# Splitting the first up- and down-weights of the ConvFFN two segments early, and moving the mixer's weight stores to GpSimd's queue

## The chip, the cores and the metric

The kernel runs on one core of one Trainium2 chip. The metric is the device time of one execution in microseconds (us). Three executions of the kernel before took 2495.51, 2503.52 and 2504.46 us; the median is 2503.52 us.

## The reference

One layer of a hybrid decoder over 2048 prompt columns and 8 sample columns, D_MODEL = 1024, D_FF = 2816, all in float32. Cut to what matters:

```python
h  = rms_norm(x, norm1) * (1 + sc1) + sh1
proj = h @ w_in                      # q, k, v | z | beta, alpha | u, v of the gating MLP
q, k, v = silu(causal_dwconv(proj_qkv, width 4))
o_a, S = gated_delta_rule(q, k, v, g, beta, s0)      # chunks, triangular solve, scan over the state S
o_a = rms_norm(o_a) * silu(z)
o_b = gelu(u) * (W_s @ rms_norm(gelu(vb)) + b)       # 128x128 mixing inside chunks
x  = x + g1 * (concat(o_a, o_b) @ w_out)
h2 = rms_norm(x, norm2) * (1 + sc2) + sh2
up = causal_dwconv(h2 @ w_up, width 3) + b
x  = x + g2 * ((silu(up[:, :D_FF]) * up[:, D_FF:]) @ w_down)
y  = rms_norm(x, final_norm)
```

## The kernel before

**Products.** A float32 product is made of three float32r products: each operand is split into a high part (a copy that rounds to float32r) and a low part (the rest). `split` does that with one ScalarE copy (L100) and one VectorE subtraction (L97). `gemm_steps` issues the three matmuls of a 128-row step on lines L119, L120 and L121. A split weight block is a tile of 128 x 2 x 512, 512 KB, high and low side by side.

**Kept weights.** A weight block is split once. `wblock(key, w, src)` splits it into the tile `w` and stores the tile to DRAM (L166, on SyncE's queue, called SP in the profile); whenever the same key comes again it loads the kept block instead (L162, on GpSimd's queue, called POOL). Segment 0 of the mixer splits all of `w_in` (48 blocks) and `w_out` (16 blocks); block 0 of the ConvFFN splits all of `w_up` and `w_down`.

**Mixer.** Four segments of 512 columns, counted 0 to 3 (segment 0 has the 8 sample columns beside them). Each one runs, in the order in which the program is written: the 12 q, k, v tiles of the input projection (`qkv_tile`) with convolution and the triangular solve (`solve_steps`, `solve_merge`); the sgu stage, four heads with one u tile and one v tile each (`sgu`, `sgu_norm`, `sgu_post`); the weave, in which the four z tiles of the projection are laid between the four steps of the state scan (`weave`, `scan`, with L575, L582, L588 and L597 to L598 as the products of a step and L579, L585 and L592 as the work between them); `gdn_post`; the load of the next segment's x (L327, SP's queue), its squares and their sum (L345, L347), a reduction over the 128 partitions by eight small products with a vector of ones (L188), the reciprocal root (`rstd_of`, L182) and its broadcast (L199); and the output projection `out_proj` with the residual stored for later (L683, L692).

**ConvFFN.** Three column blocks of 688, 688 and 680 columns. In each, 22 up-projection pairs (a gate tile and a value tile) are computed with seven half-width products of 12 matmuls a piece, on the weight blocks B11, B21, T1, T2, B22, T3, T4 of a pair. `up_weights` takes them from DRAM if they are kept; otherwise it loads 2 x 512 KB raw (L153), makes four sums and differences (L974 and the lines behind it) and splits seven blocks. After every second or third pair a down round (`down`, two blocks per down tile) adds to the output. Before the first pair, `load_h2` makes the moving operands of the first column block from the stored h2: 16 additions and subtractions of 128 x 344 (L944, L945, L951, L952) on GpSimd where `early` is set, on VectorE otherwise, and 14 splits.

**Order.** The program is built under a tile context with a scheduler that simulates a timeline and orders the instructions of every engine by it, so what is written at one place can be issued at another. Each engine then works in that order, and so does each DMA queue's issuing engine: an issue that waits for a semaphore holds up what stands behind it on that engine. GpSimd's transfers use eight semaphore lanes, so that one issue also waits until the one eight places earlier has landed. Tiles come from pools with a fixed number of buffers; an instruction that writes a tile waits until the last reader of the buffer is done. The `w` blocks have 6 buffers, the `wb` blocks of the up-projection 6, `sv` 3 and `cv` 4.

Of the kernel before, what the change touches and what calls it, by code (L numbers as in the profile page):

```python
# [9 lines left out]
F32 = mybir.dt.float32  # L10
F32R = mybir.dt.float32r
BF16 = mybir.dt.bfloat16
AF = mybir.ActivationFunctionType
ALU = mybir.AluOpType
# [11 lines left out]
FT = 22  # L26
# [19 lines left out]
def trunk(ctx, tc, A, O):  # L46
# [108 lines left out]


    kept = {}

    def wblock(key, w, src=None):

        if key in kept:
            G.dma_start(out=w, in_=kept[key])  # L162
        else:
            split(w[:, 0], w[:, 1], src)
            kept[key] = dr.tile([128, 2, 512], F32, name="kept_" + "_".join(map(str, key)))
            nc.sync.dma_start(out=kept[key], in_=w.bitcast(F32))  # L166
        return [(w[:, 0, k * 128:(k + 1) * 128], w[:, 1, k * 128:(k + 1) * 128]) for k in range(4)]

    def wpt():
# [45 lines left out]
    def nm():  # L215

        return po.tile([128, 520], F32, tag="nm", name="nm", bufs=3)
# [89 lines left out]
    def cv_slabs():  # L307
        while True:
            yield cv()[:, 0:512]
# [615 lines left out]
    def load_h2(c0, W, early=False):  # L925

        n = W // 2
        X, rest = {}, []
        eng = G if early else V
        for k in range(4):  # L930
            if k < 3 or not early:
                p, q = acct(), rawt()
# [196 lines left out]
                out=O["yT"][k * 128:(k + 1) * 128, c0 + b0:c0 + b0 + n], in_=x)  # L1129


    c = nm()[:, 0:72].rearrange("p (k c) -> p k c", k=8)
    nc.scalar.dma_start(out=c, in_=A["cT"])
    V.memset(cact, 0.0)
# [62 lines left out]
    for s in range(NSEG):  # L1197
# [36 lines left out]
        mix = mix[4:] + mix[:4]  # L1234
        pend = None
        extra = mod_half(4, cv_slabs()) if s == 0 else iter(())
        for hd in range(4):
            uv = uvt()
            sgu(0, hd, uv, h, W, extra)
            with behind():  # L1240
                if hd:
                    sgu_norm(pend)
                else:
                    v_head(3, vf[3], Z)
            sgu(1, hd, uv, h, W, extra)
            with behind():
                if hd:
                    sgu_post(hd - 1, pend, W, mix)
                else:
                    solve_merge(Z)  # L1250
            pend = uv
            if s == 0 and hd == 2:
                sk = smp_conv()
                vn, o_s, eg_s = smp_delta(sk, Z["beta"], Z["g"], states)
# [9 lines left out]
        state = Z["S"]  # L1264
        if s == 0:
            smp_mix(mix, 0, smp_gate(o_s))
        gdn_post(Z, z, W, mix)
        if s == 0:
            scale_of(s2, 32, "norm2")
# [27 lines left out]
            h2, rest = load_h2(*CB[0], early=True)  # L1297
        sq = out_proj(range(5, KT), *last, x1, acc)
        if s + 1 == NSEG:
            w0 = up_weights(0)  # L1300
        norm_h2(x1, *last[:2], (acc, sq))
    sto.close()
# [140 lines left out]
```

## Time and profile before

| | |
|---|---|
| median of three executions | 2503.52 us |
| the profiled execution's own time | 2499.25 us |
| its span, first to last instruction | 2496.5 us |
| ConvFFN block 0 (first product to the first product of block 1) | 1048.4 to 1532.8 us of the span |
| ConvFFN block 1 | 1532.8 to 1995 us |
| weave of segments 1 and 2 | some 465 to 513 and 705 to 752 us |

Times inside the profile are microseconds from the span's start. PE is TensorE's matmul stream, DVE VectorE, ACT ScalarE, POOL GpSimd, SP SyncE; a name with a q behind it (SPq) is that engine's issuing of DMAs. "Waits" are idle time of an engine just before an instruction, put down to the instruction or transfer that released it last. The granted clock (PEclk) is a share of 2.4 GHz; its low level is 1.2 GHz. GB/s is what the core's 16 DMA engines moved.

### The profile page before, as it was taken

What the parts mean: (1) busy time and instruction counts of PE and PEld (TensorE: products, weight loads), DVE (VectorE), ACT (ScalarE), POOL (GpSimd) and SP (SyncE); (2) the same over time, 40 slices, a digit from 0 to 9 for tenths busy, and PEclk for the clock granted to TensorE, in tenths of its full rate; (3) what the DMA queues carried; (4) which work ended last, traced back from release to release, by engine and by line L of the source; (5) the groups of instructions that cost most, each with busy time, mean ns of one, the idle gap of its engine ahead of it and who ended that gap; (6) DMA issues with size and microseconds to landing.
All of it is one profiled execution on the core that took longest, in us unless ns stands there. A gap on an engine that the chain in (4) does not pass through costs nothing.

```text
span 2496.5 us, 41843 instructions
## 1 busy us (share of the span) xinstructions
PE 2414.7 (97%) x15770; PEld 2240.9 (90%) x15770; DVE 1713.3 (69%) x3731; ACT 1045.9 (42%) x2128; POOL 501.3 (20%) x769
## 2 busy tenths in 40 slices
PE   7899999999999999999999999999999999999997
PEld 4798978888887878889999998999999999999997
DVE  4675668455745664799899998766655685666655
ACT  5766655456445645454444444412222242222223
POOL 0000001111201211311111112333333223333333
PEclk9999999999999999999999999999999999999998
DMA  9785787566737754888787778977777778767773
GB/s 377 243 282 170 255 306 212 153 194 202 209 113 223 222 163 143 305 327 307 280 298 295 284 287 302 319 225 237 240 228 223 223 233 296 225 212 231 227 238 116
DMA packets 224057, 600.84 MB, mean 241 GB/s; under 512 B 39345, under 2 KB 67697, under 8 KB 223345
## 3 DMA queue, kind: packets, MB, share of 16 engines
q0 software_dynamic: 84672, 308.32, 39.8%
q1 hardware_dynamic: 128672, 278.83, 31.6%
q10 hardware_dynamic: 10512, 11.04, 1.3%
q8 instruction: 124, 2.03, 0.3%
q14 instruction: 77, 0.62, 0.1%
HBM read 430.39 MB, written 167.70 MB: 240 GB/s over the span
## 4 chain that ended last, share of the span: by engine, by line
PE 75%; DVE 12%; DMA 7%; issue 3%; ACT 2%; SPq 0%; POOL 0%; ACTq 0%; DVEq 0%; POOLq 0%
PE u L119 9%; PE u L120 9%; PE u L121 9%; PE g L119 7%; PE g L120 7%; PE g L121 7%; PE d L119 6%; PE d L120 6%; PE d L121 6%; DVE acc L1021 1%; DVE cv L376 1%; DVE wb L97 1%; DVE sv L508 1%; DMA S<-in_w_down 1%; DVE TP L506 1%
## 5 line engine op out<-in xcount | busy, mean ns | idle before, releaser
L119 PE MATMUL g<-hh,w 128*128 128x512 f32 (+1 forms) x960 | 346.4, 361 | 7.7 <-ACT w L100 7.7
L1021 DVE SCALAR_TENSOR_TENSOR acc<-raw,vec,acc 128x680 f32<-128x680 f32 (+1 forms) x264 | 303.5, 1152 | 70.0 <-ACT acc L1014 67.6
L119 PE MATMUL d<-midh,w 128*128 128x344 f32 (+1 forms) x1008 | 322.2, 325 | 22.1 <-DVE xa L1087 11.9
L119 PE MATMUL u<-T,wb 128*128 128x344 f32 (+1 forms) x1056 | 338.1, 321 | 4.9 <-DMA wb<-kept_w_up_T 2.4
L121 PE MATMUL g<-hh,w 128*128 128x512 f32 (+1 forms) x960 | 341.6, 356 | 0.0
L120 PE MATMUL g<-hl,w 128*128 128x512 f32 (+1 forms) x960 | 340.6, 355 | 0.0
L120 PE MATMUL u<-T,wb 128*128 128x344 f32 (+1 forms) x1056 | 338.4, 321 | 0.3 <-DVE T L97 0.3
L121 PE MATMUL u<-T,wb 128*128 128x344 f32 (+1 forms) x1056 | 337.2, 320 | 0.9 <-DVE wb L97 0.9
L120 PE MATMUL d<-midl,w 128*128 128x344 f32 (+1 forms) x1008 | 323.7, 322 | 0.0
L121 PE MATMUL d<-midh,w 128*128 128x344 f32 (+1 forms) x1008 | 317.4, 322 | 0.4 <-DVE w L97 0.4
L1087 DVE SCALAR_TENSOR_TENSOR xa<-d,mod,xa 128x344 f32<-128x344 f32 (+2 forms) x368 | 206.1, 568 | 153.7 <-PE d L121 144.8
L1014 ACT ACTIVATE acc<-raw,vec 128x680 f32<-128x680 f32 (+1 forms) x132 | 125.9, 956 | 383.7 <-DVE raw L1009 379.1
L119 PE MATMUL u<-B,wb 128*128 128x344 f32 (+1 forms) x792 | 252.6, 320 | 2.7 <-ACT B L100 2.7
L120 PE MATMUL u<-B,wb 128*128 128x344 f32 (+1 forms) x792 | 253.1, 320 | 0.2
L121 PE MATMUL u<-B,wb 128*128 128x344 f32 (+1 forms) x792 | 252.0, 318 | 0.0
L162 POOL DMA_DIRECT2D w<-kept_w_in x144 | 76.2, 529 | 718.0 <-PE g L121 379.4
L119 PEld LDWEIGHTS d<-midh,w 128*128 128x128 f32 x1008 | 191.6, 191 | 26.6 <-issue 11.5
L119 PEld LDWEIGHTS g<-hh,w 128*128 128x128 f32 x960 | 182.9, 191 | 35.1 <-ACT w L100 8.6
L121 PEld LDWEIGHTS g<-hh,w 128*128 128x128 f32 x960 | 182.2, 190 | 28.1 <-issue 2.8
L120 PEld LDWEIGHTS g<-hl,w 128*128 128x128 f32 x960 | 182.9, 191 | 26.7 <-issue 2.0
L119 PEld LDWEIGHTS u<-T,wb 128*128 128x128 f32 x1056 | 199.4, 189 | 6.1 <-DVE sacc L1100 2.1
L121 PEld LDWEIGHTS u<-T,wb 128*128 128x128 f32 x1056 | 199.7, 189 | 1.3 <-DVE wb L97 1.2
(391 smaller groups left out, 5063.4 us busy)
## 6 DMA issues: line engine op xcount, KB each, us to landing
wb<-kept_w_up_T POOLq DMA_DIRECT2D x176, 512.0 KB, 5.0
w<-kept_w_in POOLq DMA_DIRECT2D x144, 512.0 KB, 4.0
wb<-kept_w_up_B POOLq DMA_DIRECT2D x132, 512.0 KB, 4.9
kept_w_up_T<-wb SPq DMA_DIRECT2D x88, 512.0 KB, 4.0
w<-kept_w_down POOLq DMA_DIRECT2D x88, 512.0 KB, 5.0
kept_w_up_B<-wb SPq DMA_DIRECT2D x66, 512.0 KB, 4.1
kept_w_in<-w SPq DMA_DIRECT2D x48, 512.0 KB, 4.2
w<-kept_w_out POOLq DMA_DIRECT2D x48, 512.0 KB, 4.4
```

What stands on the lines that cost most here:

```text
L97: (eng or V).tensor_tensor(out=out, in0=a, in1=hi.bitcast(F32), op=ALU.subtract)
L119: PE.matmul(ps[:, :n], wh, mh[:, c0:c0 + n], start=k == ks[0], stop=False)
L120: PE.matmul(ps[:, :n], wh, ml[:, c0:c0 + n], start=False, stop=False)
L121: pe["last"] = PE.matmul(ps[:, :n], wl, mh[:, c0:c0 + n], start=False, stop=k == ks[-1])
L162: G.dma_start(out=w, in_=kept[key])
L376: V.scalar_tensor_tensor(out=acc, in0=cr[:, j:j + SEG], scalar=vc("cqkv", ft * 4 + j), in1=acc, op0=ALU.mult, op1=ALU.add)
L506: V.tensor_tensor(out=tmp, in0=NB[:, j, j + 1:32].unsqueeze(2).to_broadcast([64, r, w]), in1=TB[:, j:j + 1, 0:w].to_broadcast([64, r, w]), ...
L508: V.tensor_tensor(out=TB[:, j + 1:32, 0:w], in0=TB[:, j + 1:32, 0:w], in1=tmp, op=ALU.subtract)
L1014: S_.activation(out=acc[:, off:W], in_=raw[:, 2:2 + m], func=AF.Identity, scale=vc("cffn", ft * 3 + 2), bias=vc("cffb", ft))
L1021: V.scalar_tensor_tensor(out=acc[:, off:W], in0=raw[:, j:j + m], scalar=vc("cffn", ft * 3 + j), in1=acc[:, off:W], op0=ALU.mult, op1=ALU.add)
L1087: V.scalar_tensor_tensor(out=xa[ft][:, b0 + o:b0 + n], in0=ps[:, o:n], scalar=mod[:, 40 + ft, 0:1], in1=xa[ft][:, b0 + o:b0 + n], op0=ALU. ...
```

## The change

Three edits. First, the stores of kept blocks go to the queue named in `keeper`: GpSimd's from the start, SP's again from just before the first `up_weights` of the ConvFFN; so 48 + 16 stores of segment 0 change their queue. Second, `prepare(s)` in segments 1 and 2 loads, adds, splits and keeps the weights of two up pairs and two down tiles each (pairs and tiles 0 and 1 in segment 1, 2 and 3 in segment 2): per segment 3 MB raw in on SP's queue, into four `cv` tiles a pair; 8 sums and differences; 18 blocks split (18 ScalarE copies and 18 VectorE subtractions) into `sv` tiles of the name `wv`; and 18 stores of 512 KB on GpSimd's queue. Four of its eight steps are written into heads 2 and 3 of the sgu stage, the rest behind the weave. Block 0 of the ConvFFN then finds these 36 blocks kept and loads them on GpSimd's queue, where it had loaded 6 MB raw, split 36 blocks and stored them. Third, the 16 additions of `load_h2` for block 0 are on VectorE (`eng = V`).

```diff
     kept = {}
+    keeper = {"q": G}
...
-            nc.sync.dma_start(out=kept[key], in_=w.bitcast(F32))
+            keeper["q"].dma_start(out=kept[key], in_=w.bitcast(F32))
...
-        eng = G if early else V
+        eng = V
...
+    def prep_block(key, src):
+        wblock(key, pa.tile([128, 2, 512], F32R, tag="sv", name="wv", bufs=3), src)
+
+    def prep_up(i):
+
+        a11, a12, a21, a22 = (cv()[:, 0:512] for _ in range(4))
+        for j, (p, q) in enumerate(((a11, a12), (a21, a22))):
+            for n, a in enumerate((p, q)):
+                nc.sync.dma_start(out=a, in_=A["w_up"][j * FT + i][:, n * 512:n * 512 + 512])
+        key = lambda n: ("w_up", i, n)
+        prep_block(key("B11"), a11)
+        prep_block(key("B21"), a12)
+        prep_block(key("T4"), a22)
+        yield
+        V.tensor_tensor(out=a22, in0=a21, in1=a22, op=ALU.add)
+        prep_block(key("T1"), a22)
+        V.tensor_tensor(out=a21, in0=a11, in1=a21, op=ALU.subtract)
+        prep_block(key("T3"), a21)
+        yield
+        V.tensor_tensor(out=a11, in0=a22, in1=a11, op=ALU.subtract)
+        prep_block(key("T2"), a11)
+        V.tensor_tensor(out=a12, in0=a12, in1=a11, op=ALU.subtract)
+        prep_block(key("B22"), a12)
+        yield
+
+    def prep_down(i):
+        for j in range(2):
+            a = cv()[:, 0:512]
+            nc.sync.dma_start(out=a, in_=A["w_down"][i][:, j * 512:j * 512 + 512])
+            prep_block(("w_down", i, j), a)
+        yield
+
+    def prepare(s):
+
+        if s in (1, 2):
+            for i in (2 * s - 2, 2 * s - 1):
+                yield from prep_up(i)
+                yield from prep_down(i)
...
+        ready = prepare(s)
         for hd in range(4):
+            if hd > 1:
+                next(ready, None)
             uv = uvt()
             sgu(0, hd, uv, h, W, extra)
...
+            if hd > 1:
+                next(ready, None)
             sgu(1, hd, uv, h, W, extra)
...
+        for _ in ready:
+            pass
         gdn_post(Z, z, W, mix)
...
         if s + 1 == NSEG:
+            keeper["q"] = nc.sync
             w0 = up_weights(0)
```

Line numbers behind the first edit are higher by one in the changed kernel (L163 is the kept load, L167 the store), and higher by more behind the new functions. PE has the same products as before.

On POOL, at the end of segment 1's projection, only loads of kept blocks stood (`w_in_14_1` is half 1 of tile 14 of `w_in`; the numbers behind a name count the tiles of the program):

```order
L162 DMA w_5941<-kept_w_in_14_1_3186 128x1024
L162 DMA w_6021<-kept_w_in_15_0_3298 128x1024
L162 DMA w_6023<-kept_w_in_15_1_3303 128x1024
L162 DMA w_6185<-kept_w_out_0_0_3513 128x1024
L162 DMA w_6187<-kept_w_out_0_1_3518 128x1024
L162 DMA w_6218<-kept_w_out_1_0_3583 128x1024
```

Now the stores of split blocks stand between the same loads (here those of pair 1 and down tile 1):

```order
L163 DMA w_6084<-kept_w_in_15_1_3303 128x1024
L167 DMA kept_w_up_1_B11_6124<-wv_6121 128x1024
L167 DMA kept_w_up_1_B21_6129<-wv_6126 128x1024
L167 DMA kept_w_up_1_T4_6134<-wv_6131 128x1024
L163 DMA w_6307<-kept_w_out_0_0_3513 128x1024
L167 DMA kept_w_up_1_T1_6140<-wv_6137 128x1024
L167 DMA kept_w_up_1_T3_6146<-wv_6143 128x1024
L167 DMA kept_w_up_1_T2_6152<-wv_6149 128x1024
L163 DMA w_6309<-kept_w_out_0_1_3518 128x1024
L167 DMA kept_w_up_1_B22_6158<-wv_6155 128x1024
L167 DMA kept_w_down_1_0_6165<-wv_6162 128x1024
L163 DMA w_6340<-kept_w_out_1_0_3583 128x1024
```

A store waits for its split on VectorE and a load for a `w` buffer that PE gives free; each of them now holds up the other kind.

On PE, behind the scan of segment 1, the sums of the next segment's squares (`c<-ones,nm`) were followed by 25 rows of the output projection (`g<-mh,w`) before the broadcast of the root (`c<-ident,rtok`):

```order
L188 MATMUL c_6115<-ones_74,nm_6112 128x1
L119 MATMUL g_6190<-mh_5216,w_6185 128x512
L120 MATMUL g_6190<-ml_5217,w_6185 128x512
L121 MATMUL g_6190<-mh_5216,w_6185 128x512
...
L119 MATMUL g_6190<-mh_5222,w_6185 128x512
L199 MATMUL c_6127<-ident_72,rtok_6124 128x128 x4
L120 MATMUL g_6190<-ml_5223,w_6185 128x512
```

Now eight rows stand between them:

```order
L189 MATMUL c_6237<-ones_74,nm_6234 128x1
L120 MATMUL g_6312<-ml_5219,w_6307 128x512
L121 MATMUL g_6312<-mh_5218,w_6307 128x512
L119 MATMUL g_6312<-mh_5220,w_6307 128x512
L120 MATMUL g_6312<-ml_5221,w_6307 128x512
L121 MATMUL g_6312<-mh_5220,w_6307 128x512
L119 MATMUL g_6312<-mh_5222,w_6307 128x512
L120 MATMUL g_6312<-ml_5223,w_6307 128x512
L121 MATMUL g_6312<-mh_5222,w_6307 128x512
L200 MATMUL c_6249<-ident_72,rtok_6246 128x128 x4
```

The broadcast comes 17 rows sooner behind the sums; the sums themselves stand 61 products behind the scan's last one, where they stood 64 to 66 behind.

On POOL, at the end of the mixer, the loads of the last `w_out` tiles stood between additions of `load_h2`, and nothing of the up-weights:

```order
L162 DMA w_10543<-kept_w_out_3_1_3831 128x1024
L944 TENSOR_TENSOR mc_10623<-acc_10617 128x344
L945 TENSOR_TENSOR mc_10624<-raw_10618,mc_10623 128x344
L951 TENSOR_TENSOR acc_10617<-raw_10618,acc_10617 128x344
L162 DMA w_10576<-kept_w_out_4_0_3938 128x1024
```

Now six blocks of pair 0 come at that place, the first down blocks and the seventh block of pair 0 behind `w_out`, and pair 1 after them:

```order
L163 DMA wb_11077<-kept_w_up_0_B11_5540 128x1024
...
L163 DMA w_11045<-kept_w_out_7_1_4435 128x1024
L163 DMA w_11551<-kept_w_down_0_0_5722 128x1024
...
L163 DMA wb_11089<-kept_w_up_0_T4_5550 128x1024
L163 DMA wb_11306<-kept_w_up_1_B11_6124 128x1024
L163 DMA wb_11308<-kept_w_up_1_B21_6129 128x1024
L163 DMA wb_11310<-kept_w_up_1_T1_6140 128x1024
L163 DMA wb_11312<-kept_w_up_1_T2_6152 128x1024
```

The load of `kept_w_up_1_B11` waits until PE has read the buffer of the first pair's second block, and PE has 24 matmuls and seven small sums between that and its first use.

## Rows read from the trace of the kernel before

**Rows 1.** The page: busy time, its share of the span and the number of instructions of each engine; the granted clock in 40 slices of the span.

```profile
PE 2414.7 (97%) x15770; PEld 2240.9 (90%) x15770; DVE 1713.3 (69%) x3731; ACT 1045.9 (42%) x2128; POOL 501.3 (20%) x769
PEclk9999999999999999999999999999999999999998
```

**Rows 2.** PE's waits from 400 to 1000 us, which hold segments 1, 2 and most of 3: who waited for whom, us in total, times, the longest.

```profile
PE c L531 <- DMA lt<-td: 3.6, 2, 2.2
PE c L473 <- DVE A L476: 2.0, 2, 1.7
```

**Rows 3.** Windows: length, busy us (and instructions) of PE, PEld, DVE, ACT and POOL, the granted clock, the DMA engines' share and GB/s. The first is pairs 0 to 3 of ConvFFN block 0, the second a stretch of block 1 with PE never idle, then the whole of block 0 and of block 1.

```profile
1048.40:1130.50 82.10, 75.36 (x458) 73.59 (x457) 78.89 (x165) 44.37 (x74) 10.07 (x7) 0.96 0.92 344
1700.00:1800.00 100.00, 100.00 (x639) 100.00 (x638) 64.01 (x103) 20.62 (x29) 32.91 (x56) 1.00 0.75 235
1048.40:1532.80 484.40, 461.44 (x2864) 457.45 (x2862) 447.73 (x903) 217.52 (x350) 67.75 (x53) 0.98 0.82 302
1532.80:1995.00 462.20, 458.00 (x2917) 456.16 (x2916) 305.37 (x539) 118.05 (x182) 145.06 (x240) 1.00 0.76 244
```

**Rows 4.** PE's four longest waits from 1048.4 to 1130.5 us (two shorter ones follow them).

```profile
PE d L119 <- ACT w L100: 2.4, 1, 2.4
PE u L119 <- DVE mc L1027: 1.7, 1, 1.7
PE u L121 <- DVE wb L97: 0.9, 1, 0.9
PE c L199 <- DVE rtok L182: 0.9, 1, 0.9
```

**Rows 5.** Groups by line and form from 1042 to 1110 us, ACT and then DVE: busy us, mean ns of one, idle before.

```profile
L100 ACT ACTIVATE wb<-S 128x512 fp32r<-128x512 f32 x12 | 7.5, 629 | 11.1 <-DVE S L981 3.9 <-PE u L121 2.5 <-DVE S L984 1.7
L97 DVE TENSOR_TENSOR wb<-S,wb 128x512 fp32r<-128x512 f32 x12 | 8.4, 703 | 0.0
```

**Rows 6.** The page's groups: the first product of the up-projection in all three blocks, with PE's idle time before it.

```profile
L119 PE MATMUL u<-T,wb 128*128 128x344 f32 (+1 forms) x1056 | 338.1, 321 | 4.9 <-DMA wb<-kept_w_up_T 2.4
```

**Rows 7.** The page's DMA issues: KB each and median us from issue to landing.

```profile
wb<-kept_w_up_T POOLq DMA_DIRECT2D x176, 512.0 KB, 5.0
w<-kept_w_in POOLq DMA_DIRECT2D x144, 512.0 KB, 4.0
kept_w_up_T<-wb SPq DMA_DIRECT2D x88, 512.0 KB, 4.0
```

**Rows 8.** Groups from 1010 to 1046 us, the stretch in which `load_h2` runs: POOL, then DVE beside it, then two DVE groups of the same shapes from 1480 to 1600 us; then the window 1010 to 1046 us.

```profile
L951 POOL TENSOR_TENSOR acc<-raw,acc 128x344 f32<-128x344 f32 x3 | 3.1, 1030 | 0.0
L97 DVE TENSOR_TENSOR B<-raw,B 128x344 fp32r<-128x344 f32 x6 | 6.6, 1120 | 0.0
L97 DVE TENSOR_TENSOR T<-mc,T 128x344 fp32r<-128x344 f32 x8 | 5.6, 696 | 0.0
L97 DVE TENSOR_TENSOR B<-acc,B 128x344 fp32r<-128x344 f32 x3 | 4.4, 1477 | 0.0
...
L97 DVE TENSOR_TENSOR T<-mc,T 128x344 fp32r<-128x344 f32 x16 | 7.8, 506 | 0.0
L97 DVE TENSOR_TENSOR B<-raw,B 128x344 fp32r<-128x344 f32 x8 | 4.6, 581 | 3.6 <-ACT B L100 3.5
...
1010.00:1046.00 36.00, 35.87 (x155) 28.71 (x154) 29.16 (x39) 14.63 (x32) 20.70 (x25) 1.00 0.84 274
```

**Rows 9.** Windows with the columns of rows 3: the weave of segment 1, the stretch behind it, the ten microseconds before the x loads at segment 1's end, and six microseconds at the start of the ConvFFN.

```profile
465.00:513.00 48.00, 48.00 (x339) 42.70 (x340) 18.61 (x43) 22.35 (x61) 4.75 (x9) 1.00 0.42 122
513.00:530.00 17.00, 17.00 (x86) 14.09 (x85) 10.46 (x29) 11.96 (x24) 2.64 (x5) 1.00 0.92 320
500.00:510.00 10.00, 10.00 (x69) 9.09 (x68) 2.19 (x6) 4.51 (x18) 0.53 (x1) 1.00 0.18 54
1050.00:1056.00 6.00, 5.90 (x43) 5.82 (x41) 6.00 (x16) 5.44 (x12) 0.00 (x0) 1.00 1.03 415
```

**Rows 10.** The timeline of POOL before 526 us (start, length, instruction, idle before it and its releaser), of SP's issue of x, of ACT's last square, of DVE's last sum and of PE's sums and broadcast.

```profile
502.93 0.53 POOL L162 DMA_DIRECT2D w<-kept_w_out  x1 [6.72 <-PE g L121]
510.22 0.53 POOL L162 DMA_DIRECT2D w<-kept_w_out  x1 [6.76 <-PE g L121]
511.76 2.25 SPq L327 DMA_DIRECT2D x<-in_xT  x4
526.05 0.62 ACT L345 ACTIVATE nm<-x 128x512 f32<-128x512 f32 x1
530.16 1.06 PE L188 MATMUL c<-ones,nm 128*128 128x1 f32 x9
537.32 1.05 PE L199 MATMUL c<-ident,rtok 128*128 128x128 f32 x8
```

**Rows 11.** The last line of the tile view of x from 500 to 548 us: us from issue to landing.

```profile
DMA to landing us min/median/max: 6.5/8.2/11.4
```

**Rows 12.** A group of DVE from 483 to 513 us, the scan of segment 1.

```profile
L592 DVE SCALAR_TENSOR_TENSOR S<-S,ed,c 128x128 f32<-128x128 f32 x16 | 4.5, 343 | 11.6 <-PE c L588 11.6
```

**Rows 13.** Waits from 0 to 300 us, segment 0: SP's largest, and PE's two largest.

```profile
SPq L166 <- DVE w L97: 94.0, 26, 13.4
PE m L266 <- ACT cact L1135: 13.0, 1, 13.0
PE g L119 <- ACT w L100: 7.7, 1, 7.7
```

## Prediction

> **What bounds the kernel now.** The first view is the page's busy times: PE works 2414.7 us of the 2496.5 us span, 97%, and its granted clock is at the high level in every slice but the last [rows 1]. So a change pays only where PE waits or runs at the low clock, and costs wherever it makes PE wait. PE's waits come next. From 400 to 1000 us, where the new work of segments 1 and 2 is put, two lines wait for 5.6 us in all [rows 2]. There is next to nothing to win there, and whatever the new work disturbs is lost. The windows of the ConvFFN show the place that can win: block 0 has PE idle for 484.40 - 461.44 = 23.0 us, block 1, which runs on kept blocks, for 462.20 - 458.00 = 4.2 us [rows 3]. Segment 0 has two long waits on other things [rows 13].
>
> **Pairs 0 to 3 of block 0.** They take 82.1 us for 458 matmuls. In a stretch of block 1 in which PE is never idle one matmul takes 100 / 639 = 0.1565 us, and 458 of them 71.7 us; 10.4 us are lost. The four longest waits are 2.4 on ScalarE's split, 1.7 and 0.9 behind VectorE, and 0.9 on the reciprocal root, 5.9 us [rows 4]; the granted clock of 0.96 is worth 0.04 x 82.1 = 3.3 us [rows 3]; the rest are small waits. VectorE is busy 78.89 of the 82.1 us, so all those waits stand behind a full queue. The change takes 36 splits of 0.70 us (25 us) and 16 sums of that size (11 us) from VectorE and 36 copies of 0.63 us (23 us) from ScalarE here [rows 5], so VectorE is left near half busy and 5.9 us of waits go. What is late next are the loads. Blocks 1 and 2 take every weight in this way, and the first product of theirs and of block 0 waits for such a load 2.4 us in all [rows 6], a small price; but at the start there is no lead: pair 1's first load waits for the buffer of pair 0's second block, and has 24 matmuls (24 x 0.1565 = 3.8 us) and seven sums before it is needed, against a landing of 5.0 us [rows 7]. I take 1 us. Raw loads and stores of the old way were 1.5 + 4.5 = 6 MB a pair, loads of the new way are 4.5 MB, and the DMA engines, at a share of 0.92 there, get easier. The clock I leave as it is, since new waits may bring it down as the old ones may have. The small waits are the rest, 10.4 - 5.9 - 3.3 = 1.2 us, and go with the others: -5.9 - 1.2 + 1 = -6. The ends are -10.4, when clock and waits both go, and -5.9 + 2 x 5.0 = +4, when pairs 0 and 1 each wait a whole landing.
>
> **The 16 additions.** VectorE takes 16 x 0.51 = 8.1 us more. But beside GpSimd's additions its own subtractions took 1.12, 0.70 and 1.48 us where the same shapes took 0.58, 0.51 (and, for the third, I take 0.58 too) later: 6 x 0.54 + 8 x 0.19 + 3 x 0.90 = 7.5 us come back [rows 8]. VectorE had 29.16 of 36 us busy there and PE 35.87. Zero, from -1 to +2. The Trainium skill ("SBUF — State Buffer", section "Who interferes with whom") says that the two engines share a port pair under an exclusive lock; the 1.12 us beside 0.58 agree with it. Without that rule the move would cost up to the 8 us that it adds to a VectorE with 7 us idle, some 1 us of PE.
>
> **Segments 1 and 2.** Each stores 18 x 0.52 = 9.4 MB and loads 3.1 MB raw. VectorE gets 18 splits and 8 sums at 0.70 us, 18 us, in a weave of 48 us where it is busy 18.6; ScalarE 18 x 0.63 = 11 us beside 22.4. The DMA engines move 122 GB/s there, and 415 GB/s were seen [rows 9], so the bulk fits. Three things may not:
>
> - *The scan.* VectorE waits for PE 11.6 us before its state updates [rows 12]: it is a chain PE, VectorE, PE with z products laid between. Splits stand right before its links, each waiting for a copy by ScalarE, which waits for one of three `sv` buffers, whose store (4.0 us to land [rows 7]) may stand on POOL's queue behind a load that waits for PE: such loads were issued at 502.93 and 510.22 us, after idle times of 6.7 and 6.8 us [rows 10]. Bounds: nothing, and one landing of 4.0 us in each of two steps. I take 1 us, because by POOL's order the stores that a split of pair 1 needs stand behind loads that PE lets go a step earlier.
> - *The x loads.* They are issued from 511.76 us, and took 6.5 to 11.4 us to land [rows 10, 11]. The stretch behind has 0.92 of the DMA engines' time taken at 320 GB/s, while the ten microseconds before had 54 GB/s [rows 9]. The stores of B22 and of the two down blocks, 1.6 MB, go out behind POOL's load at 510.22, so beside x; at 415 GB/s that is 3.8 us. The slack: the last square ended at 526.05 + 0.62 = 526.67, PE's nine sums began at 530.16 [rows 10]; they now come three to five products sooner, some 0.7 us, which leaves 2.8 us. So 1.0 us of wait; the bounds are nothing, and 4.8 us when all six last blocks (3.1 MB, 7.6 us) pass ahead of x.
> - *The root.* From the end of the sums at 531.22 to the broadcast at 537.32 us, 6.1 us, PE had 25 products, 0.24 us each [rows 10]. With eight there are 1.9 us. How long square root and reciprocal take is not to be seen but for its bound, 6.1 us, since PE did not wait: the cost is 0 to 4.2 us; I take 0.5, as the scheduler's rows behind need the result later and x is then on time or late with it.
>
> That is 2.5 us a segment, 5 for both, from 0 to 2 x 17.
>
> **Segment 0.** SP waited 94 us to store split blocks [rows 13], and raw loads stand behind those. They now go ahead. But of PE's long waits the 13.0 us are the start and the 7.7 us wait for a copy by ScalarE, whose order is the same up to there. 48 + 16 stores cost POOL issue slots of 0.53 us [rows 10] where it has little else to do. Zero, between -2 and +2.
>
> **Sum.** -6 + 0 + 5 + 0 = -1 on the profiled 2499.25 us. That execution is 4.3 us under the median of the three, which lie 9 us apart; I carry the difference over to the median, 2503.5 - 1 = 2502.5.
>
> **Rivals.**
>
> 1. *All of the loss at the start of the ConvFFN goes, and the mixer hides everything.* For it: the 14 MB of spare traffic in the weave, 29 us of idle VectorE. Against: the clock, whose dips have no shown cause there. -10.4, and -2 in segment 0: 2503.5 - 12.4 = 2491.
> 2. *Stores in the scan and beside x; slower.* Place: VectorE's splits ahead of the scan's links in segments 1 and 2. Price: two landings of 4.0 us, and 4.8 us for x, 12.8 a segment, 25.6 for both, less 6: 2503.5 + 19.6 = 2523. It decides from the point where a split ahead of a link waits for an `sv` buffer longer than the z products between the links last. For it: VectorE and POOL run in order and both wait for PE; against: the stores have 7 us between two loads of POOL and land in 4. The Trainium skill ("DMA: Bandwidth & Descriptors", section "SWDGE vs HWDGE vs iDMA") speaks for the x part: GpSimd's and SP's transfers go to different queues inside each DMA engine, which takes turns between them, so stores on GpSimd's queue would not wait for x but take a share of it; the landings of 6.5 to 11.4 us of x beside POOL's loads agree.
> 3. *The loads at the start of the ConvFFN come late.* Pairs 0 to 3 keep the time they had or lose 4 us: 2503.5 + 5 + 2 = 2510. For it: 36 loads in 80 us behind one queue whose issue waits for PE's buffers; against: the 2.4 us of rows 6.
> 4. *The splits of pairs 4 and on inherit the waits.* Pair 4 still splits seven blocks; if the pile-up only moves from pairs 0 to 3 to pairs 4 to 7, the gain is nil and the mixer's 5 us stay: 2508. Against: the splitting has 80 us of free VectorE ahead of it.
>
> **How the numbers follow.** The forecast 0.46 (2494 to 2510 by itself), rival 1 0.12, rival 2 0.17, rival 3 0.13, rival 4 0.12. A measurement of this kernel tells about 0.5%, 12.5 us, from no change, so the borders are 2491 and 2516. Faster: most of rival 1's lower half and the forecast's tail, 0.11. Slower: rival 2 but for its lower tail, and rival 3's upper tail, 0.17. Same: 0.72. The range is 2490 to 2519: a tenth of the chance lies above (half of rival 2) and less than a tenth below.
>
> **What would show it.** Right: pairs 0 to 3 take 75 to 78 us, with no PE wait on L97 or L100 and short ones on `kept_w_up`; no new wait over 1.5 us behind the scans; x landing some 3 us later; VectorE near 29 + 1 us busy in the 36 before the ConvFFN. Rival 2 shows as PE waiting for `lt`, `S` or the root, and ScalarE waiting for `kept_w_up` stores. Rival 3 shows as PE waits on `wb<-kept_w_up`; rival 4 as waits on L97 in pairs 4 to 7. The prediction is wrong if the gain at the ConvFFN's start is under 3 us or a mixer segment moves by more than 6.

## The result, and the profile after

The changed kernel is slower. Eight executions of each gave a median of 2517.63 us (2508.24 to 2527.95) against 2500.37 us (2493.40 to 2504.46); the ratio is 1.0073, with a 95% interval of 1.0060 to 1.0087. The profiled execution took 2513.29 us, its span is 2511.5 us, 15.0 us more than before. Line numbers from here on are those of the changed kernel: L576, L580, L583, L589, L593 are the scan, L626 is gdn_post, L346 and L348 are the squares of the next x and their sum.

The page's busy times and granted clock answer to [rows 1]: PE has the same work, in a longer span, and the clock is now lower in one slice of the mixer.

```profile
PE 2417.1 (96%) x15770; PEld 2243.2 (89%) x15770; DVE 1714.0 (68%) x3747; ACT 1052.2 (42%) x2132; POOL 564.4 (22%) x889
PEclk9999999989999999999999999999999999999998
```

**Where the time went.** The first product of the up-projection starts at 1076.8 us instead of 1048.4: the mixer lost 28.4 us. The ConvFFN's block 0 then takes 470.8 us instead of 484.4 and gives 13.6 back. Windows of the changed kernel (columns as in [rows 3]): scan of segment 1, the stretch behind it, pairs 0 to 3, pairs 4 to 21.

```profile
484.00:519.00 35.00, 32.07 (x218) 29.04 (x217) 21.55 (x47) 21.78 (x58) 8.58 (x16) 0.95 0.92 320
519.00:552.00 33.00, 27.00 (x114) 22.08 (x114) 15.42 (x37) 16.01 (x31) 4.84 (x9) 0.79 0.69 244
1076.80:1153.00 76.20, 72.49 (x457) 71.94 (x456) 57.77 (x125) 27.02 (x39) 20.52 (x33) 0.98 0.84 279
1153.00:1547.60 394.60, 380.94 (x2408) 379.63 (x2407) 364.18 (x735) 171.19 (x272) 60.55 (x47) 0.99 0.80 294
```

PE was busy all through the weave and the stretch behind it before, at full clock [rows 9]. Now it idles 2.9 and 6.0 us in the first two windows, and the clock of 0.79 takes 0.21 x 33 = 6.9 us more in the second.

PE's waits in segment 1, from 484 to 552 us, and in segment 2, from 737 to 798 us, where there were none before:

```profile
PE t L625 <- DVE nz L626: 3.7, 1, 3.7
PE g L119 <- ACT mh L100: 2.3, 1, 2.3
PE c L576 <- DVE S L593: 1.9, 1, 1.9
PE t L671 <- DVE uv L663: 1.0, 1, 1.0
...
PE t L625 <- DVE nz L626: 2.6, 1, 2.6
PE g L119 <- ACT mh L100: 2.0, 1, 2.0
PE c L576 <- DVE S L593: 0.9, 1, 0.9
PE c L583 <- DVE lt L580: 0.4, 1, 0.4
```

The larger two of each four belong to gdn_post: its transpose (L625) waits, and the output projection (L119) waits for its splits. Of the others, both in segment 2 and one in segment 1 (L576) are links of the scan, its chain of products and state updates; L671 belongs to the sgu stage. None names a transfer, so one goes back a step. *In the scan* the timelines of ACT and then DVE show a split whose copy waited 2.86 us until the store of an earlier block had landed and freed its `sv` buffer; the split waited for the copy, and the state update (L593) that PE needed stood behind the split:

```profile
492.54 0.63 ACT L100 ACTIVATE wv<-cv 128x512 fp32r<-128x512 f32 x1 [2.86 <-DMA kept_w_up_T<-wv]
...
493.20 0.69 DVE L97 TENSOR_TENSOR wv<-cv,wv 128x512 fp32r<-128x512 f32 x1 [1.43 <-ACT wv L100]
493.81 0.68 DVE L674 TENSOR_TENSOR uv<-uv 128x512 f32<-128x512 f32 x1
494.42 1.11 DVE L593 SCALAR_TENSOR_TENSOR S<-S,ed,c 128x128 f32<-128x128 f32 x4
```

*Behind the scan* POOL's and SP's timelines show six stores of split blocks and three `w_out` loads going out between 512 and 525 us, around x:

```profile
512.26 1.13 POOL L167 DMA_DIRECT2D kept_w_up_T<-wv  x2 [2.86 <-DVE wv L97]
514.55 0.53 POOL L167 DMA_DIRECT2D kept_w_up_T<-wv  x1 [1.16 <-DVE wv L97]
516.14 0.55 POOL L163 DMA_DIRECT2D w<-kept_w_out  x1 [1.05 <-PE g L121]
519.49 0.53 POOL L167 DMA_DIRECT2D kept_w_up_B<-wv  x1 [2.80 <-DVE wv L97]
521.73 0.53 POOL L167 DMA_DIRECT2D kept_w_down<-wv  x1 [1.71 <-DVE wv L97]
522.26 0.55 POOL L163 DMA_DIRECT2D w<-kept_w_out  x1
523.67 0.53 POOL L167 DMA_DIRECT2D kept_w_down<-wv  x1 [0.87 <-DVE wv L97]
524.40 0.55 POOL L163 DMA_DIRECT2D w<-kept_w_out  x1 [0.19 <-issue]
...
519.40 2.69 SPq L328 DMA_DIRECT2D x<-in_xT  x4
```

The same four loads of x were issued from 511.76 us before [rows 10] and took 6.5 to 11.4 us [rows 11]. Now the tile view of x and ACT's waits from 519 to 545 us say:

```profile
DMA to landing us min/median/max: 11.1/15.8/19.7
...
ACT nm L346 <- DMA x<-in_xT: 6.3, 3, 2.7
ACT nm L343 <- DMA x<-in_xT: 3.2, 1, 3.2
```

So the last x lands at 521.4 + 19.7 = 541.1 us, 16 us later than before. The squares stand on ACT between the splits of gdn_post, so both wait.

Two smaller places: in the last output projection PE waits once for `w_out`, whose loads stand behind those of pair 0's blocks; and in pairs 0 to 3 the waits of [rows 4] are down to two. Waits of PE from 1015 to 1077 us, then from 1077 to 1160 us:

```profile
PE g L119 <- DMA w<-kept_w_out: 3.0, 1, 3.0
...
PE u L119 <- DVE mc L1028: 2.8, 1, 2.8
PE u L119 <- DVE rtok L183: 0.9, 1, 0.9
```

### The profile page after: what moved, and what is told of

Read it like the earlier page. It is cut to its first block, busy times and chain, and to the rows that moved or that the text cites. A ratio compares the mean times of both kernels' runs of the same rounds, so it can differ in the third digit from the quotient of the medians.

```text
span 2511.5 us, 41978 instructions
## 1 busy us (share of the span) xinstructions
PE 2417.1 (96%) x15770; PEld 2243.2 (89%) x15770; DVE 1714.0 (68%) x3747; ACT 1052.2 (42%) x2132; POOL 564.4 (22%) x889
## 3 DMA queue, kind: packets, MB, share of 16 engines
q1 hardware_dynamic: 115424, 226.40, 25.9%
## 4 chain that ended last, share of the span: by engine, by line
PE 72%; DVE 11%; DMA 10%; ACT 3%; issue 3%; SPq 1%; POOL 1%; ACTq 0%; DVEq 0%; POOLq 0%
PE u L119 9%; PE u L120 9%; PE u L121 9%; PE g L119 7%; PE g L121 7%; PE g L120 7%; PE d L119 6%; PE d L121 6%; PE d L120 6%; DMA x<-in_xT 1%; DVE acc L1022 1%; DMA S<-in_w_down 1%; DVE wb L97 1%; DVE sv L509 1%; DVE TP L507 1%
## 5 line engine op out<-in xcount | busy, mean ns | idle before, releaser
L119 PE MATMUL g<-hh,w 128*128 128x512 f32 (+1 forms) x960 | 347.2, 362 | 8.4 <-ACT w L100 7.7
L119 PE MATMUL u<-T,wb 128*128 128x344 f32 (+1 forms) x1056 | 337.6, 321 | 6.0 <-DMA wb<-kept_w_up_T 2.9
L119 PE MATMUL d<-midh,w 128*128 128x344 f32 (+1 forms) x1008 | 318.1, 321 | 16.4 <-DVE xa L1088 10.8
L119 PE MATMUL u<-B,wb 128*128 128x344 f32 (+1 forms) x792 | 252.8, 320 | 5.2 <-ACT B L100 4.2
L119 PEld LDWEIGHTS g<-hh,w 128*128 128x128 f32 x960 | 182.6, 190 | 36.8 <-ACT w L100 8.2
L119 PEld LDWEIGHTS d<-midh,w 128*128 128x128 f32 x1008 | 189.1, 189 | 18.9 <-issue 10.3
L119 PEld LDWEIGHTS u<-T,wb 128*128 128x128 f32 x1056 | 199.0, 189 | 7.2 <-DVE mc L1028 3.1
L120 PEld LDWEIGHTS u<-T,wb 128*128 128x128 f32 x1056 | 199.3, 189 | 0.6 <-DVE T L97 0.5
L121 PEld LDWEIGHTS u<-T,wb 128*128 128x128 f32 x1056 | 199.3, 189 | 0.0
```

The lines of the kernel that those rows point to most:

```text
L119: PE.matmul(ps[:, :n], wh, mh[:, c0:c0 + n], start=k == ks[0], stop=False)
L120: PE.matmul(ps[:, :n], wh, ml[:, c0:c0 + n], start=False, stop=False)
L121: pe["last"] = PE.matmul(ps[:, :n], wl, mh[:, c0:c0 + n], start=False, stop=k == ks[-1])
```

## The experiments

Single profiles differ by the moments at which the clock fell, by 26 to 47 us of span in all, so the stretches are compared without it: the length of a stretch, from one product of PE to another, less half of the time for which the granted clock was at 1.2 GHz in it. "Scan 1" and "scan 2" go from a scan's first product to its last state product, "scan 0" from its first product to the first product of the output projection. "Behind" is from the last state product of the scan to the last product of that output projection; "out 3" is from segment 3's last state product to the first up product.

| us without the clock's loss | scan 0 | scan 1 | behind 1 | scan 2 | behind 2 | out 3 | block 0 |
|---|---|---|---|---|---|---|---|
| before | 50.6 | 29.8 | 90.9 | 29.8 | 90.9 | 57.5 | 472.4 |
| changed | 52.3 | 32.9 | 95.8 | 31.9 | 94.8 | 60.2 | 465.7 |
| e1 no preparation | 51.9 | 29.8 | 90.9 | 29.8 | 90.9 | 57.2 | 472.1 |
| e2 splits only | 52.8 | 33.9 | 90.9 | 34.1 | 90.9 | 57.2 | 473.6 |
| e3 stores only | 52.6 | 29.6 | 90.9 | 31.5 | 90.9 | 57.2 | 477.0 |
| e4 one pair | 52.1 | 32.4 | 90.9 | 30.6 | 90.9 | 60.0 | 471.5 |
| e5 fewer stores | 51.9 | 33.7 | 90.9 | 31.9 | 90.9 | 59.6 | 477.6 |
| e6 w_out first | 52.1 | 33.4 | 98.1 | 31.4 | 97.1 | 57.2 | 467.6 |
| e7 in the output projection | 52.4 | 29.8 | 90.9 | 29.8 | 90.9 | 57.2 | 466.7 |
| e8 stores on SP | 50.6 | 37.8 | 93.9 | 33.3 | 94.0 | 59.8 | 466.3 |
| e9 squares last | 52.1 | 33.2 | 96.0 | 30.7 | 96.2 | 60.0 | 466.3 |
| e10 segment 0 on SP | 50.6 | 29.8 | 91.1 | 29.8 | 90.9 | 57.2 | 466.9 |

The stretches between these (the projections of q, k, v and the solve, and the rest of segment 0) differ by up to 8 us from profile to profile, more in e11, and nothing is read from them. All stretches but scan 0, and scan 1 of e8, hold the same products in every row. Scan 0 holds eight products more in the nine rows from 51.9 us up: a group of sixteen (`t<-slab`) that began ahead of the scan's first product before (at 216.6 us, the scan at 220.15) now follows it (at 220.0 us, the scan at 219.26). The sixteen keep PE busy for 3.0 us, so some 1.5 us of the difference is order and not loss. The tile view of `slab` from 200 to 300 us, before and changed:

```profile
L801 PE MATMUL t<-slab,sv x16: 592/822/1059, 216.6 to 222.5; 128*32 128x512 f32 x16
```

```profile
L802 PE MATMUL t<-slab,sv x16: 592/604/617, 220.0 to 223.8; 128*32 128x512 f32 x16
```

In the changed kernel the clock took 1.7 us in scan 1, 6.8 behind it, 3.4 behind scan 2 and 5.1 in block 0; before, nothing in the first three and 11.9 in block 0.

**e1, no preparation.**

```diff
-        if s in (1, 2):
+        if s in ():
```

> The changed kernel without the preparation in segments 1 and 2 (the stores of segment 0 on GpSimd's queue and the 16 additions on VectorE stay). If the preparation is what costs (either theory below): first up product at 1048 us (+-4) instead of 1076.8, ConvFFN block 0 at 484 us again, time 2500 +-4. If the queue of the stores in segment 0 or the moved additions cost: first up product over 1054 us, time over 2506.

2502.15 us, ratio to before 0.9987 (0.9971 to 1.0002). The first up product came at 1058.6 us, later than expected, but 6.9 us of that is the clock and the rest lies in stretches that nothing is read from; all stretches of the table but scan 0 are as before. The loss is the preparation's.

**e2, splits without stores; e3, stores without splits; e4, one pair a segment.**

```diff
 e2
-        wblock(key, pa.tile([128, 2, 512], F32R, tag="sv", name="wv", bufs=3), src)
+        w = pa.tile([128, 2, 512], F32R, tag="sv", name="wv", bufs=3)
+        split(w[:, 0], w[:, 1], src)
 e3
-        wblock(key, pa.tile([128, 2, 512], F32R, tag="sv", name="wv", bufs=3), src)
+        d = dr.tile([128, 2, 512], F32, name="trial_" + "_".join(map(str, key)))
+        G.dma_start(out=d, in_=src.unsqueeze(1).to_broadcast([128, 2, 512]))
 e4
-            for i in (2 * s - 2, 2 * s - 1):
+            for i in (s - 1,):
```

> The preparation loads raw weights and splits them, but stores nothing, so the ConvFFN splits them again (work done twice). Theory traffic (the stores share the DMA engines with the x loads and keep the three sv buffers, PE waits behind late x): no stores, so x lands in under 10 us at the median (15.8 in the changed kernel), first up product at 1048 to 1056 us, time 2500 to 2508. Theory engines (splits on VectorE and ScalarE stand ahead of the scan's links and of gdn_post): first up product at 1068 us or later, time 2515 or more.

> The preparation loads the raw weights and stores 512 KB per block straight from the raw tile, with no split; the stored blocks are used by nobody and the ConvFFN splits as before. Theory traffic: x lands in 12 us or more at the median, first up product at 1062 to 1077 us, time 2512 to 2528. Theory engines: first up product at 1048 to 1054 us, time 2500 to 2506.

> One pair and one down tile each in segments 1 and 2 (pairs 0 and 1 kept), so that all nine stores go out before the last w_in load and none beside x. Theory traffic: x lands in 9 us or less at the median, first up product at 1048 to 1056 us, and ConvFFN block 0 at 474 to 480 us (half of the 13.6 us or more): time 2493 to 2502. Theory engines: half of the mixer's loss stays, first up product at 1062, time 2507.

e2: 2513.35 us, 1.0042 (1.0019 to 1.0065). e3: 2510.66, 1.0023 (1.0004 to 1.0042). e4: 2508.70, 1.0018 (0.9995 to 1.0041). Neither pure theory held. Splits alone make the scans 4 us longer and leave x and the stretch behind them untouched; stores alone leave scan 1 and both stretches behind untouched, since they wait for no split and are gone before x. They lengthen scan 2 by 1.7 us, and block 0, whose work is that of before, by 4.6, which nothing here explains. Only both together make x late. The tile view of x from 505 to 552 us, in e2 and in e3:

```profile
DMA to landing us min/median/max: 5.7/8.7/12.0
```

```profile
DMA to landing us min/median/max: 6.3/8.1/10.9
```

In e2 the scan's links wait with no store about, as DVE's timeline shows: the state update (L593), for which PE waited 1.8 us, stands behind a split and a difference of the preparation, and the next link (L580) behind three more:

```profile
500.00 0.68 DVE L97 TENSOR_TENSOR wv<-cv,wv 128x512 fp32r<-128x512 f32 x1
500.60 0.68 DVE L1153 TENSOR_TENSOR cv<-cv 128x512 f32<-128x512 f32 x1
501.20 1.12 DVE L593 SCALAR_TENSOR_TENSOR S<-S,ed,c 128x128 f32<-128x128 f32 x4
502.23 0.68 DVE L674 TENSOR_TENSOR uv<-uv 128x512 f32<-128x512 f32 x1
502.83 0.68 DVE L97 TENSOR_TENSOR wv<-cv,wv 128x512 fp32r<-128x512 f32 x1
503.44 0.68 DVE L1155 TENSOR_TENSOR cv<-cv 128x512 f32<-128x512 f32 x1
504.04 0.68 DVE L97 TENSOR_TENSOR wv<-cv,wv 128x512 fp32r<-128x512 f32 x1
504.64 0.68 DVE L580 TENSOR_TENSOR lt<-ve,c 128x512 f32<-128x512 f32 x1
```

So the wait for a store's landing, seen in the changed kernel, isn't needed: the splits' place in VectorE's order is enough. In e4 x and the stretches behind the scans are those of before, as the theory of traffic has it, but the first up product at 1064.2 us and the time are near what the theory of engines named. The scans (+2.6 and +0.8) and out 3 (+2.5) still lost 5.9 of the 15.8 us by which that product is later; 3.5 are the clock, and the rest lies in stretches that nothing is read from. Block 0, 478.3 us as measured, is only 0.9 under before without the clock.

**e5, the last six stores of each segment left out** (pairs 1 and 3 are then split again in the ConvFFN).

```diff
-        if ("w_up", i, "T4") in kept:
+        if ("w_up", i, "B22") in kept:
...
+        if key[1] % 2 and key[-1] not in ("B11", "B21", "T4"):
+            w = pa.tile([128, 2, 512], F32R, tag="sv", name="wv", bufs=3)
+            return split(w[:, 0], w[:, 1], src)
```

> All splits stay, but the last six blocks of each segment (T1, T3, T2, B22 and both down blocks of the second pair) are not stored; pairs 1 and 3 split them again in the ConvFFN. Theory late stores (the x loads are late because stores that waited for splits and buffers go out beside them): x lands in 10 us or less at the median (15.8 in the changed kernel), the stretch from the last scan product to the last product of the output projection, less what the clock took, is 91 to 92 us in segments 1 and 2 (95.8 and 94.8 in the changed kernel, 90.9 before), while the scans keep 31 to 34 us (29.8 before); time 2500 to 2510. Theory engines (the order of splits on VectorE and ScalarE makes the wait behind the scan too): the stretch stays at 94 us or more, time 2512 or more.

2506.36 us, 1.0017 (0.9998 to 1.0035). With the splits in place and only those stores gone, x lands in segment 1 as soon as before and the stretch behind is 90.9 us to the tenth, clock included, while the scans stay long. So the theory of late stores holds. The tile view of x:

```profile
DMA to landing us min/median/max: 5.6/7.1/9.1
```

**e8, all kept stores on SP's queue.**

```diff
-    keeper = {"q": G}
+    keeper = {"q": nc.sync}
```

> The changed kernel with all kept stores on SP's queue, those of the preparation too. Theory late stores (bytes beside x, whichever queue): stretch behind the scans 94 us or more less the clock, time 2510 to 2522. Rival queue (GpSimd's stores take turns with SP's x loads, and hold up the w loads behind them): x lands in 10 us or less from its issue, scans 31 us or less, time 2508 or less.

2513.61 us, 1.0046 (1.0028 to 1.0065). x took 12.5 us at the median, the stretches behind are 93.9 and 94.0, at the edge of the theory's 94: most of the wait is there on either queue. With the stores on x's own queue x landed 3 us sooner. That fits the rule on turns that the prediction cited (the Trainium skill, "DMA: Bandwidth & Descriptors", section "SWDGE vs HWDGE vs iDMA"), but it doesn't isolate it, since the two down stores now go out behind x, at 525.78 and 527.79 us. The scans got worse, 37.8 (some 1.7 us of it twelve products of the sgu stage that run in it here) and 33.3, and scan 0 is 50.6 us again.

```profile
DMA to landing us min/median/max: 9.7/12.5/14.5
```

**e9, the squares of x behind gdn_post on ACT and DVE.**

```diff
+            pv, pq = pe["sa"], pe["sv"]
             c0, W, x = load_x(s + 1)
-            h = norm_h(x, W, norm_sum(x, W))
+            with tc.issue_after(pv.ins), tc.issue_after(pq.ins):
+                r = norm_sum(x, W)
+            h = norm_h(x, W, r)
```

(`pv` and `pq` are the last copy and the last subtraction of gdn_post, which `split` notes in lines left out here.)

> The changed kernel with the squares of the next x (ScalarE) and their sums (VectorE) ordered behind the last split of gdn_post in every segment; splits and stores of the preparation unchanged, so x stays late. Theory in-order queues (PE waits behind the scan because gdn_post's multiplications and splits stand behind squares that wait for x): PE's waits on nz and mh behind the scans go, the stretch behind the scan less the clock falls from 95.8 and 94.8 to 91-93 us, time 2505 to 2512, though x still takes 14 us or more to land at the median. Rival (PE needs x itself, through sums and root): a wait of 4 us or more turns up at the sums or the broadcast, the stretch stays over 94 us, time 2515 or more.

2519.02 us, 1.0060 (1.0042 to 1.0079): the theory fell, and the rival holds in size, though at another place. The waits on nz and mh are gone, but the stretches stay at 96.0 and 96.2, because PE then runs out of output projection and waits for x itself, at the gates' products of the next segment (PE's waits from 770 to 810 us; segment 1 has the same 2.3 us):

```profile
PE g L394 <- ACT x L706: 2.3, 1, 2.3
```

That wait is about half of the 5 us. Of the other half some 1.7 us lie in the gates' 16 small products, which PE runs in four pieces with 5.0 us in all in segment 1, where before it ran two with 3.3; the rest is open.

**e6, w_out's loads first.**

```diff
-            G.dma_start(out=w, in_=kept[key])
+            pe["load"] = G.dma_start(out=w, in_=kept[key])
...
-            w0 = up_weights(0)
+            with tc.issue_after(pe["load"].ins):
+                w0 = up_weights(0)
```

> The changed kernel with the loads of pair 0's kept blocks ordered behind the last w_out load on GpSimd. Theory: the 3.0 us wait for w_out in the last output projection goes, its stretch (last scan product to first up product, less the clock) falls from 60.2 to 57.2-57.8 us, pairs 0 to 3 stay at 74 to 76 us; time 3 us under the changed kernel, 2514. Rival: pair 0's loads come late instead, the stretch falls but pairs 0 to 3 take 3 us more; time 2517.

2520.34 us, 1.0069 (1.0051 to 1.0087). Out 3 fell from 60.2 to 57.2 as expected, and pairs 0 to 3 took 78.6 us instead of 76.2, at the same clock. That is the rival in size, but its cause is not shown, since none of PE's waits from 1023 to 1160 us is for a load:

```profile
PE d L119 <- ACT midh L100: 2.6, 1, 2.6
PE u L119 <- ACT mc L1027: 2.1, 1, 2.1
PE c L200 <- DVE rtok L183: 0.6, 1, 0.6
```

The stretches behind the scans are 2.3 us longer than in the changed kernel, though the edit leaves them alone; that is open.

**e12, the 16 additions back on GpSimd** (`eng = G if early else V`).

> The changed kernel with the 16 additions of load_h2 back on GpSimd. Theory (the move is worth nothing, VectorE's subtractions get back what it takes over): subtractions of 128 x 344 beside the additions take 0.7 to 1.5 us again (0.5 to 0.6 in the changed kernel), the stretch from the last scan product to the first up product 59.5 to 61 us less the clock (60.2 in the changed kernel), time 2512 to 2522. Rival (the move pays, since GpSimd's additions would stand between the loads of w_out and of pair 0): stretch 62 us or more, time 2522 or more.

2525.60 us, 1.0090 (1.0059 to 1.0121), which overlaps the changed kernel's interval. Out 3 is 58.9 us, a little under the changed kernel, so the move didn't pay. The time is the rival's, but its stretch is not, and why it is above the theory's is open. DVE's subtractions took 0.64 and 1.10 us in two of their groups, and 0.51 in every group of the changed kernel (first row e12, second the changed kernel):

```profile
L97 DVE TENSOR_TENSOR B<-mc,B 128x344 fp32r<-128x344 f32 x3 | 3.2, 1101 | 0.3 <-ACT B L100 0.3
```

```profile
L97 DVE TENSOR_TENSOR B<-mc,B 128x344 fp32r<-128x344 f32 x3 | 1.5, 512 | 0.0
```

The squares' sums on VectorE (L348), 0.69 us each in the changed kernel, paid more: one took 7.16 us in e12, while GpSimd ran seven additions one behind the other. DVE's timeline, then the window of those additions (columns as in [rows 3]; POOL is busy all through it):

```profile
1055.88 7.16 DVE L348 TENSOR_TENSOR nm<-nm 128x512 f32<-128x512 f32 x1 [0.28 <-ACT nm L346]
```

```profile
1055.67:1062.48 6.81, 5.35 (x24) 4.05 (x23) 6.61 (x1) 2.46 (x7) 6.79 (x8) 1.00 1.13 411
```

**e7, the preparation in the output projection.** Each step is ordered behind a residual addition (L694, `res`) of the output projection of segments 1 and 2; w_out's loads first as in e6.

```diff
-            if hd > 1:
-                next(ready, None)
...
+        with tc.issue_after(pe["res"].ins):
+            next(ready, None)
         if s + 1 < NSEG:
             Zn = gates(s + 1, x, W)
...
             out_proj((ft,), *last, x1, acc)
+            with tc.issue_after(pe["res"].ins):
+                next(ready, None)
...
```

> The same preparation, but each step ordered behind a residual addition of the output projection of segments 1 and 2 (so no split in the scan and no store beside x), and the w_out loads first as in the run before. Theory place (the work costs only where it stands ahead of the scan's links and beside x): scans 29.8 us, the stretch behind them 90.9 to 92 us, ConvFFN block 0 less the clock 466 us (472.4 before): 6 us under the kernel before, ratio 0.996 to 0.999. Theory amount (18 splits and 12 MB a segment cost PE waits wherever they stand): 2508 or more, ratio over 1.002.

2493.78 us, 0.9971 (0.9954 to 0.9987): 0.3% faster than the kernel before, with the same splits, the same bytes and the same stores as the changed one. The profiled execution, 2502.85 us, is among the slowest of the twelve: without the clock's loss its stretch ahead of segment 0's scan took 221.4 us, against 213.2 to 216.3 in the other profiles. So the time is read from the twelve, and from the profile only the stretches. The scan of segment 1 and the stretch behind it, in windows:

```profile
501.60:531.40 29.80, 29.80 (x215) 27.55 (x214) 11.58 (x30) 15.18 (x44) 1.69 (x4) 1.00 0.44 129
531.40:622.30 90.90, 90.90 (x442) 72.72 (x441) 60.79 (x143) 61.56 (x125) 20.75 (x39) 1.00 0.84 285
```

PE never idles, at full clock, though the DMA engines move 285 GB/s in the second window and most of the 18 splits run in it (from 565.9 to 642.8 us).

**e10, e7 with segment 0's stores on SP; e11, that with two pairs in segment 0 too.**

```diff
 e10
-    keeper = {"q": G}
+    keeper = {"q": nc.sync}
...
+        if s:
+            keeper["q"] = G
         ready = prepare(s)
 e11
-        if s in (1, 2):
-            for i in (2 * s - 2, 2 * s - 1):
+        if s < 3:
+            for i in (2 * s, 2 * s + 1):
...
```

(In e11 the stores of the preparation stay on GpSimd's queue; those lines are left out.)

> The run with the preparation in the output projection, and the 64 stores of segment 0 back on SP's queue. Theory: the scan of segment 0, which took 51.9 to 52.8 us in five of the runs with these stores on GpSimd and 50.6 with them on SP, is 50.6 us again: 1.5 us under that run, ratio to the kernel before 0.995 to 0.998. Rival: SP's stores hold up raw loads and residual stores, no gain, 0.998 to 1.000.

> As the run before, with two pairs prepared in the output projection of segment 0 too, so that pairs and down tiles 0 to 5 are kept. Theory: each prepared pair is worth 1.5 to 1.7 us in the ConvFFN, block 0 less the clock falls from 466 to 463 us, ratio 0.993 to 0.997. Rival: in segment 0, where VectorE still splits w_out and w_in, the two pairs more cost PE waits of 3 us or more, and the ratio is 0.997 or above.

e10: 2495.29 us, 0.9970 (0.9955 to 0.9986), the same as e7; scan 0 is 50.6 us again, with the eight products out of it, and the time shows no gain from it. e11: 2531.42 us, 1.0105 (1.0081 to 1.0129): the rival holds, by more than it named. After segment 0's output projection PE waits for the modulation weights and for VectorE (waits from 360 to 410 us), and block 0 took 468.7 us less the clock, no gain over four pairs.

```profile
PE t L445 <- DVE lt L858: 7.0, 2, 6.7
PE m L293 <- DMA slab<-in_w_mod: 3.8, 2, 3.1
```

## Why the prediction was wrong

Forecast was 1 us less; measured were 17.3 us more between the medians. The 2517.63 us lie under the upper end of the range, 2519, only because rival 2 had been allowed for there.

- **ConvFFN, -6: right in size.** Block 0 fell by 6.7 us without the clock, and by 13.6 with it. The seven profiles with four pairs kept have 465.7 to 467.9 us there, the six with fewer or none 471.5 to 477.6. Pairs 0 to 3 took 76.2 us, inside the 75 to 78 named, and the kept loads made no wait there, where 1 us was taken. But 1.7 of these 5.9 us are the clock: 4.2 us were gained there and 2.6 in the pairs behind. Of the 5.9 us of waits that were to go, 3.7 us were still there, one of them longer than before (`mc`, 2.8 us for 1.7). The gain that the clock added (11.9 to 5.1 us lost) was left at zero.
- **The 16 additions, 0: right** by e1 and e12, with the contention as stated and, in e12, a sum of squares held up for longer than any row of before shows.
- **Segments 1 and 2, +5: this step failed.** The two scans and the stretches behind them cost 3.1 + 4.9 + 2.1 + 3.9 = 14.0 us, and the clock 11.9 more, 25.9 us against 5. Part by part:
  - *The scan, 1 us a segment:* 3.1 and 2.1. The reason given (a split waiting for an `sv` buffer) occurs, but e2 shows that splits ready in VectorE's queue do it as well.
  - *x, 1 us:* 4.9 and 3.9, the bound of 4.8 that was named and not taken. The sum counted "the stores of B22 and of the two down blocks" beside x; POOL's timeline above shows T1, T3 and T2 going out too, 5 to 7 us ahead of x. e5, which leaves all six out, shows that the six make x late, not how much is whose. The parts were priced as if they were independent: in e2 and e3 x is on time with splits or with stores alone, and late only with both.
  - *The root, 0.5 us:* nothing; PE never waited for the broadcast there.
  - *The clock:* no term at all in the mixer. Behind the waits it was low for 13.6 us in segment 1 and 6.8 in segment 2, which nearly doubled the price of the waits. That is not an accident of the profiled execution: the mean granted clock of the changed kernel's eight executions is 0.984, that of the kernel before 0.987 in the executions beside the experiments, and 0.003 x 2510 = 7.5 us (an estimate) is some two fifths of the 17.3 us between the medians.
- **Segment 0, 0: no loss shown.** Scan 0 is 1.3 to 2.2 us longer in all nine rows of the table with the stores of segment 0 on GpSimd, and 50.6 us again with SP (e8, e10), but 1.5 us of that are the eight products more; e7 and e10 take the same time.
- **Not seen:** out 3, +2.7 us and 1.7 of clock, from pair 0's loads ahead of w_out's. They stood in the order that the section on the change quotes. In e6, with the order turned round, the wait goes and pairs 0 to 3 take 2.4 us more.
- **The measured sum:** -6.7 + 14.0 + 2.7 = 10.0 us without the clock. The clock took 39.9 us of the span instead of 34.9, 12.0 more in the mixer and 7.0 less behind it. Together these are the 15.0 us of the span.
- Rival 2 named the mechanism, the place and the side, and was given 0.17. That its 25.6 us for both segments meet the 25.9 measured is luck: it priced no clock, and the waits alone are 14.0. The evidence for it was at hand: the splits stood directly before the links in VectorE's order, and a stretch with 0.92 of the DMA engines' time taken has no room for 3 MB.

## What to carry to other kernels

Work that is hidden by the sum of idle time isn't hidden by place: put it where PE has long products of its own and nothing waits for the engines that do the work (e7), not between the links of a chain (e2) or beside a load that is needed next (e5). When several parts of one stretch are each near their limit, price the case in which they come together, and take that bound: splits alone (e2) and stores alone (e3) left x on time. A wait of PE of several us can cost as much again in granted clock, so a forecast that adds waits needs a term for it.

## What the runs showed of the hardware

- A 512 KB load's landing grew with what was under way and not with its own size: 8.2 us at the median beside w_out's loads, 15.8 with six stores more, three just ahead of x and three beside it. DMA view of the changed kernel from 512 to 545 us, GB/s in 40 slices: near 400 for most of it.

```profile
GB/s 119 171 276 400 405 407 350 263 298 328 300 348 353 258 370 422 420 417 417 407 392 395 425 412 410 397 397 397 397 397 395 405 397 204 57 20 0 0 0 0
```

- The granted clock fell to its low level after PE's waits behind the scans in the changed kernel and in e6 and e12, each time in both segments, for 6.8 to 13.6 us. In e5, e7 and e10, which have no such wait, it stayed at 2.4 GHz through the same stretches. In e8 and e9, with waits of 2.0 to 2.8 us, it fell in three of four, for 3.4 to 6.8 us. In every profile it also fell within the first 100 us, near the ends of blocks 0 and 1 of the ConvFFN and at the end of the span; the other falls differ from profile to profile.
- A VectorE sum of 128x512, 0.69 us in the changed kernel, took 7.16 us in e12 beside seven GpSimd additions that left no gap between them.
